# A later place for the mLSTM's output splits, and two more PSUM banks for the input projection

## The chip, the cores and the metric

The kernel runs on one core of a Trainium2 chip. The metric is the device time of one execution in microseconds. TensorE does matrix products into PSUM (8 banks of 128 partitions x 512 fp32 values), VectorE and ScalarE read PSUM and work elementwise, GpSimd helps with elementwise work on SBUF, and SyncE (SP) issues the DMAs. The page calls the engines PE (its weight loads PEld), DVE, ACT, POOL and SP.

## What is computed

One layer of a streaming encoder on a sequence of 1024 tokens with 1024 features, in fp32:

```
x = x + 0.5 * swiglu_ffn(x, ffn1...)
h = rms_norm(x, mix_norm)
(aq, ak, av, iq, ik, iw, mx, mv, mi, mf, mo, ga, gb) = split_columns(h @ w_in)
ya = dsa_attention(q, k, v, iq, ik, iw)      # top-k keys by an indexer's score, then softmax
yb = mlstm_branch(mx, mv, mi, mf, mo, ...)   # matrix memory, chunk by chunk, gated by mo
merged = sigmoid(ga) * (ya @ w_proj_a) + sigmoid(gb) * (yb @ w_proj_b)
x = x + merged @ w_out
x = x + 0.5 * swiglu_ffn(x, ffn2...)
```

## The kernel before

Every fp32 product is made of three faster ones: each operand is split into a rounded part hi and a rest lo (ScalarE copies hi, VectorE or GpSimd subtracts for lo), and `mm3` (lines 831 to 833) adds hi x hi, hi x lo and lo x hi in PSUM. The products with large weights follow a scheme of 2x2 blocks with seven products in place of eight.

The input projection h @ w_in is the generator `mixing`. Its work is a written-out list, `MIXING`, of items (p, q): p is a pair of 128-column blocks of w_in (MX0, MX1, MV0, MV1, AKV, AQ0, AQ1, G_A[0], G_A[1], MO0, MO1, G_B[3], and at last G_A[2] and G_A[3] together), q one of the seven products. An item is 12 matmuls of 128x512 (four steps of `mm3`) into one bank. Products 0 and 1 of a pair share a bank, 5 and 4 as well, and 6 and 3; the second of each adds to what the first left, after VectorE or ScalarE has read the first's sum. A middle pair runs in the order 5, 6, 1, 4, 2, then product 0 of the next pair, then 3. G_A[2] and `LAST` = G_A[3] run side by side in the order 0, 1, 5, 4, 6, 3, 2. The token operands lie in SBUF pages named h (products 0, 1, 2, 6), swap (5, 4) and side (3).

An item that begins a bank takes the first of the list `self.banks`, and one that ends a bank appends it: a queue of free banks. It holds four: 0, 1, 6 and 7. Banks 2 and 3 serve transposes and small products, and banks 4 and 5 hold the output of the mLSTM's current chunk (`out` in `mlstm`), and later attention's scores.

The weights of an item are loaded into a page "raw", then split into one of four pairs of slots in the page "round" by ScalarE (line 570) and GpSimd (571); with `LOOK = 3` the split of an item is written three items ahead, just before the matmuls of the third item before it. Products 5, 6, 4, 2 of some pairs come ready split from DRAM (567).

Beside the projection run other generators: the mLSTM scan over eight chunks (`mlstm`), and the top-k search for attention (`topk`, lines 1605 to 1699, mostly VectorE). `pump` moves the projection by half an item, counts a tick, and calls what `later(n, f)` has put n ticks ahead. `mlstm` pumps as it goes, and returns four items short of (G_A[1], 3). Hooks are called behind certain items of `LAST`. Behind (LAST, 1) `load_yb` starts the loads of the mLSTM's gated output (eight blocks of 128x512, line 1979, one a tick), and four ticks behind each load `halves` splits the block into the page h0 (ScalarE line 960, VectorE 961). Behind (LAST, 4) the query loads are written (2107), behind (LAST, 3) the key loads (2112).

Then attention follows. In its gaps `proj_b` multiplies the split output with w_proj_b (loads of its gate at line 2000, the sums times the gate at 2007, weight splits at 191).

The order in each engine's queue is not the order of the source. The program is built with `schedule_with_timeline_sim=True`: a planner runs through an estimate of its own, and gives an engine that comes free one of the instructions that are ready by the estimate, the earliest in the source first. On the chip each queue then runs in the order so fixed. A tile's buffers are taken from SBUF in source order, the one that has been free longest first.

Lines of use below: 1268 is the sum of a finished corner in `mixing` (VectorE), 1302 the sum behind product 5, 1307 the one behind product 4, 1266 and 1275 ScalarE's copies behind products 1 and 0, 1940 the scaling of a chunk's output in `mlstm` (the last reader of banks 4 and 5), 1966 the gating of the mLSTM's output (`gated`), 2043 the normed keys in `keys_norm`, 2055 the stores of the keys to `d_kg`, 1409 the stores of gates.

Of the kernel before, what the change touches and what calls it, by code (L numbers as in the profile page):

```python
# [744 lines left out]
class Block:  # L745
# [1225 lines left out]
    def load_yb(self):  # L1971

        nc = self.nc
        self.segment("h0", None)
        self.ybT = [[None, None] for _ in range(4)]
        def part(i):
            th, h = i // 4, i % 4
            t = self.ar.alloc(512)
            nc.sync.dma_start(t.f, self.d_yb[h, :, th * 512:th * 512 + 512])

            def halves():
                hi, lo = self.take("h0", 512), self.take("h0", 512)
                self.split(hi.r, lo.r, t.f)
                t.free()
                self.ybT[h][th] = hi, lo
            self.later(4, halves)


        for i in range(8):
            self.later(i, lambda i=i: part(i))  # L1990

# [330 lines left out]
    def run(self, x, out):  # L2322
# [66 lines left out]
        def used(*qs):  # L2389
            for q in qs:  # L2390
                for pair in T[q]:
                    for b in pair:
                        b.free()
# [9 lines left out]
        def third_used():  # L2403
            used(3)
            self.key_loads()
            self.w.prime(3, 1)

        self.hooks = {(LAST, 1): first_used, (LAST, 4): sums_used, (LAST, 2): lambda: used(6, 2),
# [14 lines left out]
        self.pump_waiting()  # L2423
        self.rq = ar.alloc(64, keep=True)
        self.mlstm((G_A[1], 3))
        self.pump_past((G_A[1], 3))
        assert not self.waiting
        self.close("extra")
# [76 lines left out]
```

## Time and profile before

| | |
|---|---|
| median of 3 runs | 2098.55 us (2096.47 to 2101.47) |
| the profiled execution | 2095.19 us, span 2093.1 us |
| TensorE clock granted over it | 0.996 of full |
| TensorE busy | 2035.2 us, 97% |
| VectorE busy | 1615.8 us, 77% |
| ScalarE busy | 1047.7 us, 50% |
| GpSimd busy | 303.3 us, 14% |
| DMA, share of 16 engines | 52.4% on SP's queue, mean 175 GB/s |

Busy time counts an instruction's own span. A matmul's shown duration overlaps the next one's, so a steady stream of 128x512 products is read from its starts. The span runs from the first instruction to the last; the execution's time has 2.1 us around it. The mLSTM's last chunks, the projection's end and the start of attention lie between 1060 and 1200 us of the span. The granted clock of TensorE is given as a share of full speed: 1.00 is 2.4 GHz, 0.50 is 1.2 GHz.

### The profile page before, as it was taken

The page shows a single profiled execution, that of the slowest core. Times are in us where ns is not written, and L with a number is a line of the kernel's source. Part 1 is how long each engine was busy: PE and PEld are TensorE (multiplying, and loading weights), DVE is VectorE, ACT ScalarE, POOL GpSimd, SP SyncE. Part 2 cuts the span into 40 slices and gives each one's busy share as a digit, 9 for nine tenths or more (in the row PEclk, how much of TensorE's full clock was granted, in tenths as well). Part 3 has the DMA queues.
Part 4 walks back from the last instruction along what each step waited for, and adds up shares of the span by engine and source line. Part 5 has one row for each costly group of instructions (what it writes and reads, how often), then busy time and mean ns, then how long its engine had stood idle before and what let it go on. Part 6 is the DMA issues. An engine that isn't in the chain of part 4 may idle for free.

```text
span 2093.1 us, 27987 instructions
## 1 busy us (share of the span) xinstructions
PE 2035.2 (97%) x9341; PEld 1669.1 (80%) x9341; DVE 1615.8 (77%) x2847; ACT 1047.7 (50%) x1961; POOL 303.3 (14%) x353
## 2 busy tenths in 40 slices
PE   7999999999999989999998999999999999999999
PEld 5788887888887777788787788788888888888887
DVE  7987888979866576988888489798976676669863
ACT  8332433334437566976775378636533333334442
POOL 1000000000004222223523445322000000000000
PEclk9999999999999999999999999999999999999999
DMA  5477778895543262576676912832332323386331
GB/s 187 128 247 225 255 258 280 275 362 183 174 185 136 56 192 86 156 219 196 200 254 212 324 51 70 299 115 96 123 125 101 111 97 105 107 294 247 126 111 40
DMA packets 286604, 366.63 MB, mean 175 GB/s; under 512 B 22924, under 2 KB 172028, under 8 KB 286332
## 3 DMA queue, kind: packets, MB, share of 16 engines
q1 hardware_dynamic: 286460, 364.85, 52.4%
q8 instruction: 73, 1.20, 0.2%
q14 instruction: 71, 0.58, 0.1%
HBM read 245.72 MB, written 119.05 MB: 174 GB/s over the span
## 4 chain that ended last, share of the span: by engine, by line
PE 52%; DVE 5%; DMA 4%; ACT 2%; issue 1%; SPq 0%; POOL 0%; DVEq 0%; ACTq 0%; POOLq 0%
PE psum L832 15%; PE psum L831 15%; PE psum L833 15%; PE psum L2161 1%; PE psum L1535 1%; PE psum L1536 1%; PE psum L2216 1%; PE psum L2215 1%; DMA round<-d_s 1%; DMA extra<-d_w 1%; DVE plain L1646 0%; DMA d_tb<-plain 0%; DVE plain L1565 0%; DVE h L961 0%; ACT plain L1676 0%
## 5 line engine op out<-in xcount | busy, mean ns | idle before, releaser
L831 PE MATMUL psum<-h,round 128*128 128x512 f32 x656 | 260.9, 399 | 5.6 <-ACT round L570 2.7
L832 PE MATMUL psum<-h,round 128*128 128x512 f32 x656 | 258.7, 395 | 1.0 <-DVE h L961 0.8
L833 PE MATMUL psum<-h,round 128*128 128x512 f32 x656 | 257.6, 394 | 0.8 <-POOL round L571 0.5
L831 PEld LDWEIGHTS psum<-h,round 128*128 128x128 f32 x656 | 123.8, 189 | 33.8 <-ACT round L570 3.7
L833 PEld LDWEIGHTS psum<-h,round 128*128 128x128 f32 x656 | 123.6, 188 | 28.3 <-issue 1.4
L832 PEld LDWEIGHTS psum<-h,round 128*128 128x128 f32 x656 | 124.0, 189 | 26.5 <-DVE h L961 1.6
L831 PE MATMUL psum<-swap,round 128*128 128x512 f32 x328 | 131.0, 400 | 6.7 <-DVE plain L1648 2.0
L833 PE MATMUL psum<-swap,round 128*128 128x512 f32 x328 | 131.1, 400 | 0.5 <-POOL round L571 0.5
L832 PE MATMUL psum<-swap,round 128*128 128x512 f32 x328 | 130.0, 396 | 0.8 <-DVE swap L961 0.6
L571 POOL TENSOR_TENSOR round<-raw,round 128x512 fp32r<-128x512 f32 x73 | 102.4, 1409 | 163.0 <-ACT round L570 137.9
L1646 DVE TENSOR_SCALAR_CACHE_REDUCE plain<-plain 128x384 bf16<-128x384 f32 (+1 forms) x124 | 107.7, 868 | 2.1
L960 ACT ACTIVATE round<-plain 128x512 fp32r<-128x512 f32 x73 | 45.7, 631 | 99.1 <-PE psum L832 93.8
L303 ACT ACTIVATE round<-plain 128x512 fp32r<-128x512 f32 x75 | 46.9, 631 | 89.9 <-PE psum L832 60.7
L833 PE MATMUL psum<-h,extra 128*128 128x512 f32 x212 | 82.5, 390 | 1.5 <-POOL extra L571 1.5
L831 PEld LDWEIGHTS psum<-swap,round 128*128 128x128 f32 x328 | 62.7, 192 | 23.2 <-ACT plain L1677 2.4
L831 PE MATMUL psum<-side 128*128 128x512 f32 x208 | 80.9, 389 | 0.0
L832 PE MATMUL psum<-side 128*128 128x512 f32 x208 | 80.9, 389 | 0.0
L833 PE MATMUL psum<-side 128*128 128x512 f32 x208 | 80.9, 389 | 0.0
L832 PE MATMUL psum<-h,spare 128*128 128x512 f32 x196 | 76.6, 391 | 1.9 <-DVE h L961 1.9
L831 PE MATMUL psum<-h,extra 128*128 128x512 f32 x192 | 75.0, 391 | 3.3 <-DVE plain L1123 3.3
L914 POOL MEMSET raw<- 128x384 f32 x1 | 0.4, 419 | 533.0 <-DMA d_o<-plain 533.0
L831 PE MATMUL psum<-h,spare 128*128 128x512 f32 x196 | 76.8, 393 | 0.4 <-ACT h L960 0.4
(770 smaller groups left out, 5916.1 us busy)
## 6 DMA issues: line engine op xcount, KB each, us to landing
plain<-d_a SPq DMA_DIRECT2D x154, 256.0 KB
d_a<-plain SPq DMA_DIRECT2D x126, 256.0 KB
d_s<-plain SPq DMA_DIRECT2D x93, 256.0 KB
raw<-in_ffn_w_gate_dram SPq DMA_DIRECT2D x44, 512.0 KB
h<-in_ffn_w_down_dram SPq DMA_DIRECT2D x66, 256.0 KB
plain<-in_w_in_dram SPq DMA_DIRECT2D x32, 512.0 KB
round<-d_s SPq DMA_DIRECT2D x64, 256.0 KB
raw<-in_w_in_dram SPq DMA_DIRECT2D x57, 256.0 KB
```

The costliest lines, as they stand in the source:

```text
L303: k.nc.scalar.activation(hi.r.rearrange("p (k c) -> p k c", k=4), src, AF.Copy)
L571: k.nc.gpsimd.tensor_tensor(lo.r, raw.f, hi.f, ALU.subtract)
L831: mm(ps, lhs[0], rhs[0], start=start, stop=False, skip_group_check=more)
L832: mm(ps, lhs[0], rhs[1], start=False, stop=False, skip_group_check=more)
L833: mm(ps, lhs[1], rhs[0], start=False, stop=stop, skip_group_check=more)
L960: self.split_A = self.nc.scalar.activation(hi, src, AF.Copy).ins
L1535: self.nc.tensor.matmul(o, qb, khi.r[:, s * n:s * n + n], start=True, stop=False)
L1536: last = self.nc.tensor.matmul(o, qb, klo.r[:, s * n:s * n + n], start=False, stop=True).ins
L1646: v.tensor_scalar(s.junk[:, :s.width[j]], s.sc[j], one(s.cand, j), one(s.neg, j), ALU.is_ge, ALU.add, accum_out=one(s.cnt, j))
L2161: self.last = nc.tensor.transpose(ps[:, j * P:(j + 1) * P], pr[j].f[:, kt * P:(kt + 1) * P], self.ident).ins
L2215: mm(po, vr[:, kt, g, :], hi.r, start=kt == 0, stop=False)
L2216: mm(po, vr[:, kt, g, :], lo.r, start=False, stop=kt == b)
```

## The change

Two things. The eight `halves` are no longer put four ticks behind their loads; they are collected in `self.yb_halves` and called in the hook of (LAST, 3), behind the key loads and ahead of the weights of the next stage. Only two items of the projection come after this hook in the source, (G_A[2], 2) and (LAST, 2), and their weights are split by then. And when `mlstm` returns, banks 4 and 5 are appended to the projection's queue of free banks, which then holds six.

```diff
@@ load_yb
                 self.ybT[h][th] = hi, lo
-            self.later(4, halves)
+            self.yb_halves.append(halves)
 
+        self.yb_halves = []
         for i in range(8):
             self.later(i, lambda i=i: part(i))
@@ run
         def third_used():
             used(3)
             self.key_loads()
+            for halves in self.yb_halves:
+                halves()
             self.w.prime(3, 1)
@@ run
         self.mlstm((G_A[1], 3))
+
+        self.banks += [4, 5]
         self.pump_past((G_A[1], 3))
```

## Rows read from the trace of the kernel before

**Rows 1.** The page, its first lines: the span, then busy us of each engine.
```profile
span 2093.1 us, 27987 instructions
PE 2035.2 (97%) x9341; PEld 1669.1 (80%) x9341; DVE 1615.8 (77%) x2847; ACT 1047.7 (50%) x1961; POOL 303.3 (14%) x353
```

**Rows 2.** Windows: stretch, its us, busy us (instructions) by engine, clock, DMA, GB/s.
```profile
1100.00:1120.00 20.00, 20.00 (x90) 16.57 (x89) 19.97 (x30) 14.56 (x29) 4.07 (x3) 1.00 0.77 252
1120.00:1140.00 20.00, 17.85 (x80) 13.66 (x79) 19.96 (x21) 7.14 (x13) 13.24 (x7) 1.00 0.34 106
...
1180.00:1200.00 20.00, 16.76 (x75) 12.99 (x74) 8.93 (x19) 6.38 (x11) 7.03 (x11) 1.00 0.82 292
```

**Rows 3.** TensorE's timeline: start, us, line, operands; in brackets idle before and its releaser.
```profile
1004.93 0.47 PE L831 MATMUL psum<-swap,round 128*128 128x512 f32 x1 [2.02 <-DVE plain L1648]
...
1065.65 0.39 PE L831 MATMUL psum<-swap,round 128*128 128x512 f32 x1
...
1071.09 0.39 PE L831 MATMUL psum<-h,round 128*128 128x512 f32 x1
...
1125.35 0.47 PE L831 MATMUL psum<-h,round 128*128 128x512 f32 x1 [1.20 <-DVE plain L837]
...
1145.97 0.47 PE L831 MATMUL psum<-swap,round 128*128 128x512 f32 x1 [1.36 <-DVE plain L1302]
...
1148.57 0.39 PE L833 MATMUL psum<-swap,round 128*128 128x512 f32 x1
1151.64 0.80 PE L831 MATMUL psum<-h,round 128*128 128x512 f32 x1 [2.69 <-ACT round L570]
```

**Rows 4.** ScalarE's timeline; between the first two rows five more splits of line 960.
```profile
1147.84 0.63 ACT L960 ACTIVATE h<-more 128x512 fp32r<-128x512 f32 x1 [2.81 <-DMA more<-d_yb]
...
1150.98 1.66 ACT L570 ACTIVATE round<-raw 128x512 fp32r<-128x512 f32 x3
...
1156.59 0.63 ACT L960 ACTIVATE h<-spare 128x512 fp32r<-128x512 f32 x1 [3.95 <-DMA spare<-d_yb]
```

**Rows 5.** The chain that ended last, from 1136 to 1152: start, us, what.
```profile
1142.09 5.72 DMA more<-d_yb
```

**Rows 6.** Windows around the wait before 1151.64; columns as in rows 2.
```profile
1149.00:1151.60 2.60, 0.00 (x0) 0.00 (x0) 2.60 (x5) 2.60 (x6) 0.00 (x0) 0.91 1.05 406
1151.60:1153.00 1.40, 1.36 (x3) 1.16 (x4) 1.20 (x3) 1.03 (x2) 1.33 (x2) 0.50 1.05 405
1153.00:1155.00 2.00, 2.00 (x7) 1.54 (x6) 1.09 (x2) 0.00 (x0) 2.00 (x2) 0.61 1.06 388
```

**Rows 7.** VectorE's timeline, columns as in rows 3.
```profile
1071.29 0.69 DVE L1302 TENSOR_TENSOR more<-spare,psum 128x512 f32<-128x512 f32 x1 [0.39 <-PE psum L833]
...
1073.33 0.69 DVE L1940 TENSOR_TENSOR spare<-psum,plain 128x512 f32<-128x512 f32 x1
...
1081.99 0.75 DVE L1966 SCALAR_TENSOR_TENSOR spare<-more,par,spare 128x512 f32<-128x512 f32 x1 [1.33 <-ACT spare L1965]
...
1089.61 0.75 DVE L1966 SCALAR_TENSOR_TENSOR plain<-plain,par 128x512 f32<-128x512 f32 x1 [1.98 <-DMA plain<-d_h]
...
1124.55 0.65 DVE L1307 TENSOR_TENSOR more<-more,psum 128x512 f32<-128x512 f32 x1
...
1131.29 2.25 DVE L2043 TENSOR_TENSOR plain<-plain 128x1024 f32<-128x1024 f32 x1
...
1151.81 0.69 DVE L1302 TENSOR_TENSOR spare<-plain,psum 128x512 f32<-128x512 f32 x1 [0.20 <-DMA d_kg<-spare]
...
1175.09 0.69 DVE L2007 TENSOR_TENSOR plain<-plain,psum 128x512 f32<-128x512 f32 x1 [2.03 <-PE psum L833]
```

**Rows 8.** SP's timeline of DMA issues, from 1150 to 1160.
```profile
1153.04 1.04 SPq L2000 DMA_DIRECT2D plain<-d_tb  x2
...
1156.95 2.92 SPq L2107 DMA_DIRECT2D swap<-d_aq  x4
```

## The prediction

> **What bounds the kernel now.** The page comes first: one core, a span of 2093.1 us, TensorE busy for 97% of it [rows 1]. A gain can only come from stretches in which TensorE stands still, so I read the windows by stage for the part that the diff touches, from the mLSTM's last chunks (about 1060 us) to the start of attention (about 1175 us). From 1100 to 1140 us VectorE is busy for 39.9 of 40 us, while TensorE falls from 20.00 to 17.85 us in the second half [rows 2]: the end of the input projection is bound by VectorE, which still finishes the top-k search, and TensorE has slack there. Then the list of TensorE's waits, and the timeline for what ended each. Three of them matter [rows 3]: 1.20 us before 1125.35, 1.36 us before 1145.97, 2.69 us before 1151.64.
>
> The last one ends with a weight split: the first of the three L570 that start at 1150.98 ends at 1151.6. In front of them on ScalarE stand six splits of the mLSTM's output (L960), and the first of these had waited 2.81 us for its load [rows 4], which was issued at 1142.09 and took 5.72 us [rows 5]. After the wait the clock is at half: a granted share of 0.50 over 1.40 us and of 0.61 over 2.00 us [rows 6], a loss of 0.50 x 1.40 + 0.39 x 2.00 = 1.5 us. So this place holds 2.7 + 1.5 = 4.2 us, 0.2% of the time, which is also about what a measurement of this kernel can tell from no change.
>
> **Part one, the splits.** Nothing is added or removed: eight splits, each one L960 on ScalarE and one L961 on VectorE, move from four half steps behind their loads to the hook of (LAST, 3). They stay hidden: 8 x 0.63 = 5 us of ScalarE, which stands idle 3.95 us before 1156.59 alone [rows 4], and the first product that needs them is multiplied at 1175.09 [rows 7]. Without that cover they would cost up to 5 us at the start of attention. The loads stay where they are, and no DMA changes its place. Eight 128x512 buffers are held until the hook, but the destinations of the two L1302 that matter below are allocated before any of the eight was freed, so those stay as they are.
>
> The question is whether the move in the source moves them in the queue. A queue's order is the planner's, which gives a free engine whatever is ready by its estimate; the source only sets who goes first among the ready. The trace shows how far it reaches: on SP the loads of proj_b (L2000) stand at 1153.04, before the query loads (L2107) at 1156.95 [rows 8], which the source has first, in the hook of (LAST, 4). And it shows that the place in the source did not put the six L960 first: with `LOOK = 3` the split of the weights of (G_A[2], 6) is written before the matmuls of (LAST, 5), the first two `halves` behind them. It had the better claim and stands behind all six, so by the estimate it wasn't ready (it needs the slots of (G_A[2], 5)) and ScalarE was free. A lower claim for the six doesn't change that. I take 0 us for part one; the other bound is that the order does change.
>
> If it does, something else is late next. (G_A[2], 4) ends at 1148.57 + 0.23 = 1148.8 [rows 3]. Of the items behind it, (LAST, 4) needs the second L1302, which waited until 1151.81 for the d_kg store to leave its destination and ends at 1152.5 [rows 7]. If the planner fills the time with all of (G_A[2], 6) and then (LAST, 6), the whole 4.2 us are won; the 1.36 us before 1145.97 stay, since they end with the first L1302. If it keeps the present order, four matmuls of (G_A[2], 6) and then (LAST, 4), TensorE waits until 1152.6 all the same, and (LAST, 4) is done 12 x 0.227 = 2.7 us later at 1155.3, or 1156.8 with the half clock; now it is done by 1156.95, when the loads that overwrite its operand start [rows 8]. So: -4.2 to 0 us.
>
> **Part two, the banks.** They are appended when the mLSTM returns, four items short of (G_A[1], 3). At that point two of the projection's four banks are free; (G_A[1], 2) and (MO0, 0) take those, and the next two, banks 4 and 5, go to (MO0, 5) and (MO0, 6). Both still hold the last chunk's output: it is read until L1940 ends at 1073.33 + 0.69 = 1074.0 [rows 7], while (MO0, 5) starts at 1065.65 [rows 3]. So the change adds a wait at the mLSTM's end. Queued behind it on TensorE is the rest of the projection; the four pairs of weight slots let only (G_A[1], 3) and (MO0, 1) pass it, 24 matmuls at (1071.09 - 1065.65) / 24 = 0.227 us [rows 3], done by 1071.1. Then TensorE stands until 1074.0: 2.9 us. The low bound: without the L1302 of (MO0, 5) before it (0.69 us and a wait of 0.39 us [rows 7]) L1940 can end at 1072.9, which leaves 1.8 us. The high bound adds the half clock, 1.5 us, as after the wait of 2.69 us, behind which a matmul took 0.80 us; behind the 2.02 us before 1004.93 it took 0.47 us [rows 3]. So 1.8 to 4.4 us late; I take 3, nearest to L1940's row.
>
> What becomes of it: VectorE follows TensorE there, but stood idle 1.33 us before 1081.99 and 1.98 us before 1089.61 [rows 7]; 3.0 - 3.3 leaves about 0 for VectorE, and at most 4.4 - 3.3 = 1.1. (The second of these is a wait for the mLSTM's last output, whose transposes can now run earlier, in the gap.) TensorE's own delay runs into its waits for VectorE, 1.2 + 1.4 us up to 1146, and then into the 2.7 us at the splits. So the 3 us are absorbed, and the end moves by VectorE's shift, 0 to 1.1 us; I take 0.5.
>
> The gain: the wait before 1125.35 is one for a bank. (LAST, 0) takes the one that (G_B[3], 4) gave back, which the L1307 at 1124.55 still reads (L837 right behind it is only the last VectorE instruction done by then) [rows 3, 7]. With two more banks it goes, 1.2 us. But L2043, whose product TensorE transposes next, ends at 1131.29 + 2.25 = 1133.5 on a VectorE that is full [rows 2, 7], so TensorE only waits longer there: I take 0, with 1.2 as the other bound.
>
> The Trainium skill, "TensorE: Matmul & The Clock Gate", section "HAM oscillation — how this bites in real kernels", tells of a kernel in which double-buffering PSUM, on top of a mended feed, gave no further gain; that speaks against the banks. By it this term is 0, by the row 1.2 us. The 0 in the sum comes from L2043, and the sum stands without the page.
>
> **Sum.** 0 (splits) + 0.5 (wait at the mLSTM's end) - 0 (bank wait) = +0.5 us on an execution of 2095.2 us (span 2093.1 [rows 1] and 2.1 around it). The median of the runs, 2098.55, stands 3.4 us above that execution, so 2099 us.
>
> **Rivals.**
> *Queue kept, wait absorbed* (0.58), as worked out; with the runs' own spread 2096 to 2102 us. In it the first half of the diff does not do what it says.
> *The splits do leave ScalarE's way* (0.24). For it: the chain of waits goes from the d_yb load through the L960 to L570 and TensorE [rows 4, 5]. Against it: the planner's order, and the second L1302. -4.2 us, and with the bank's 1.2 us -5.4: 2093 to 2098 us, 2095 in the middle.
> *The new wait is not absorbed* (0.18), the one on the slower side. If the planner expects L1940 late, it puts more of the top-k search ahead of VectorE's reads of (MO0, 5) and what follows; the idle 3.3 us are then used up before TensorE's delay arrives, and a full VectorE [rows 2] carries the rest to the end. It decides once VectorE is more than 3.3 us late. Against it: the search was paced by the projection's own sums so far. +1.8 to +4.4 us, and 1.5 us more if a later wait halves the clock again: 2100 to 2105 us.
>
> The range, 2093 to 2104 us, holds all but the ends of the second and third. Beside these three, the planner also rewrites attention's queues, whose first 20 us hold 3.2 us without TensorE [rows 2]; that may be won or lost again, and I give it a sixth of the first case, half to each side. Faster by over 0.2% (4.2 us): the better two thirds of the second and the lucky part of the first, 0.16 + 0.05 = 0.21. Slower by as much: the upper two thirds of the third and the unlucky part, 0.12 + 0.05 = 0.17, which I round to 0.20 for mechanisms that I don't see. Within: 0.59.
>
> **What would show it.** Right: ScalarE still runs L960 ahead of L570 near 1148, and TensorE waits there; (MO0, 5) starts behind L1940, after a TensorE wait of 2 to 3 us near 1072; no bank wait near 1125 and a longer one for L2043. Wrong: L570 ahead of the L960 and no wait over 1 us from 1145 to 1160 (the second rival); VectorE full from 1080 on and every later wait at its old length (the third); or other waits in attention, which I hold fixed.

## The result

The change makes the kernel slower: 2108.6 us median of 5 runs (2105.19 to 2113.88) against 2096.47 us for the kernel before on the same chip (5 runs, 2091.11 to 2101.47). The ratio is 1.0056, with a 95% interval of 1.0030 to 1.0082: 11.7 us, 6 to 17. The profiled execution is the longest of the five, 2113.88 us.

**Profile after.** Line numbers below the first hunk are two higher than before (L2000 is L2002, L2043 is L2045). First the page's span and busy times, against [rows 1].

```profile
span 2111.9 us, 27973 instructions
PE 2042.6 (97%) x9341; PEld 1673.6 (79%) x9341; DVE 1618.7 (77%) x2847; ACT 1048.7 (50%) x1961; POOL 300.8 (14%) x353
```

The span is 18.8 us longer. Some of that was there before the touched code was reached. TensorE's timeline after begins with a row that answers to the first one of [rows 3]; up to this point both kernels have the same instructions in the same order.

```profile
1011.98 0.47 PE L831 MATMUL psum<-swap,round 128*128 128x512 f32 x1 [2.03 <-DVE plain L1648]
...
1069.62 0.60 PE L1385 MATMUL psum<-ident,more 128*128 128x128 f32 x4
...
1080.41 0.63 PE L1385 MATMUL psum<-ident,spare 128*128 128x128 f32 x4 [1.99 <-DVE spare L1940]
...
1088.24 0.50 PE L831 MATMUL psum<-swap,round 128*128 128x512 f32 x1 [1.73 <-DVE more L1302]
...
1143.83 1.09 PE L1385 MATMUL psum<-ident,plain 128*128 128x128 f32 x8 [0.97 <-DVE plain L2045]
...
1156.05 0.47 PE L831 MATMUL psum<-swap,round 128*128 128x512 f32 x1 [1.19 <-DVE plain L1302]
...
1161.63 0.68 PE L831 MATMUL psum<-h,round 128*128 128x512 f32 x1 [2.58 <-ACT round L570]
...
1185.10 1.07 PE L1535 MATMUL psum<-side,swap 128*128 128x512 f32 x4
...
1187.95 0.50 PE L1535 MATMUL psum<-side,swap 128*128 128x512 f32 x1 [0.87 <-DVE plain L2149]
1190.63 0.70 PE L1535 MATMUL psum<-side,swap 128*128 128x512 f32 x2 [1.49 <-DVE plain L2153]
1191.83 0.73 PE L1536 MATMUL psum<-side,swap 128*128 128x512 f32 x2 [0.49 <-DMA side<-d_kg]
1194.24 0.77 PE L1535 MATMUL psum<-side,swap 128*128 128x512 f32 x1 [1.33 <-DMA swap<-d_aq]
1198.13 0.80 PE L1535 MATMUL psum<-side,swap 128*128 128x512 f32 x1 [1.84 <-DVE plain L2149]
...
1362.80 0.80 PE L832 MATMUL psum<-swap,round 128*128 128x512 f32 x1 [0.65 <-DVE swap L961]
```

The wait for L1648 ends at 1011.98 in place of 1004.93 [rows 3], so about 7 us belong to this execution and not to the change. To leave them out, I measure two stretches between rows that every variant has: from the mLSTM's transposes (the L1385 at 1069.62) to attention's first score (L1535), and from there to a wait of the merge behind attention (the L832 at 1362.80). The same three rows of TensorE's timeline before, and two of its waits there that are compared below:

```profile
1062.44 0.60 PE L1385 MATMUL psum<-ident,more 128*128 128x128 f32 x4
...
1133.60 1.09 PE L1385 MATMUL psum<-ident,plain 128*128 128x128 f32 x8 [0.28 <-DVE plain L2043]
...
1174.89 1.07 PE L1535 MATMUL psum<-side,swap 128*128 128x512 f32 x4
...
1196.75 0.50 PE L1535 MATMUL psum<-side,swap 128*128 128x512 f32 x1 [2.07 <-DVE plain L2147]
...
1343.00 0.80 PE L832 MATMUL psum<-swap,round 128*128 128x512 f32 x1 [0.58 <-DVE swap L961]
```

The projection's end went from 112.45 to 115.48 us (+3.0), attention from 168.11 to 177.70 us (+9.6). The sum, 12.6 us, is what the runs measure within their interval. Three quarters of it lie in attention, whose own code the diff does not touch. (A program that was traced twice, e1 and e3 below, gave -0.2 and -0.3 us for the first stretch and +9.5 and +9.0 for the second; so the stretches of one execution are good to about half a microsecond, where the order of the instructions is the same.)

**The projection's end.** The predicted wait is there: 1.99 us for L1940, behind which (MO0, 5) follows, then a second one of 1.73 us for the L1302 that reads (MO0, 5). The bank wait before 1125 is gone, and TensorE waits longer for the normed keys (0.97 us against 0.28 in the same place before). ScalarE runs in the old order:

```profile
1157.83 0.63 ACT L960 ACTIVATE h<-more 128x512 fp32r<-128x512 f32 x1 [2.57 <-DMA more<-d_yb]
...
1160.96 1.65 ACT L570 ACTIVATE round<-raw 128x512 fp32r<-128x512 f32 x3
```

The six splits still stand ahead of the weight split, and TensorE still waits 2.58 us there [rows 3, 4].

**Attention's start.** SP's issues of proj_b's first two gate loads, and the first sum that needs one (VectorE), after:

```profile
1175.59 0.32 SPq L1409 DMA_DIRECT2D d_sa<-plain  x1
1175.96 0.42 SPq L2002 DMA_DIRECT2D plain<-d_tb  x1
...
1185.76 0.32 SPq L1409 DMA_DIRECT2D d_sa<-plain  x1
1186.95 0.32 SPq L2002 DMA_DIRECT2D plain<-d_tb  x1
```
```profile
1199.13 0.68 DVE L2009 TENSOR_TENSOR plain<-plain,psum 128x512 f32<-128x512 f32 x1
```

Before, both loads were issued at 1153.04 [rows 8] and the first sum ran at 1175.09 [rows 7]. With the 10 us by which everything is later at this point (the L570 wait ends at 1161.63, before at 1151.64), the loads are some 13 and 24 us late and the sum 14. In VectorE's queue the sum now stands behind five score reductions (L2149); before, it stood ahead of the first. By the order of allocations in the source, the first load now gets the buffer out of which a gate of G_A[2] is stored (L1409), the second the one of G_A[2]'s sum behind product 5 (L1302): both are in use until the projection's end. proj_b has one bank, so its second block of 12 matmuls waits for that sum. In the kernel before the blocks of proj_b stood between the score pairs; now only scores are left there, and TensorE waits five times within 11 us: by the rows above three of these waits end with VectorE, which has to read the banks of earlier scores, and two with loads of the keys (`side`) and queries (`swap`). The clock falls. Windows after, columns as in [rows 2]:

```profile
1185.00:1190.00 5.00, 3.27 (x14) 2.05 (x12) 2.05 (x3) 1.33 (x2) 0.27 (x2) 1.00 1.02 414
1190.00:1195.00 5.00, 2.55 (x8) 1.58 (x9) 1.89 (x6) 2.11 (x3) 2.74 (x4) 0.75 1.00 370
1195.00:1200.00 5.00, 3.16 (x8) 1.96 (x7) 3.31 (x7) 2.09 (x5) 1.65 (x3) 0.50 1.05 379
1200.00:1205.00 5.00, 5.00 (x19) 4.13 (x18) 1.47 (x4) 2.36 (x4) 3.60 (x4) 0.73 0.91 287
```

The theory from this (A): the late splits do nothing to ScalarE's queue, but they give their eight input buffers back later in the source, so that the gate loads are handed other buffers, which come free late; and the wait for L1940 is carried to the end. Its rival (B): the banks do it all, since attention's scores meet other banks.

### The profile page after: what moved, and what is told of

Same layout as the page of the kernel before. It is cut to its first block, busy times and chain, and to the rows that moved or that the text cites. A ratio compares the mean times of both kernels' runs of the same rounds, so it can differ in the third digit from the quotient of the medians.

```text
span 2111.9 us, 27973 instructions
## 1 busy us (share of the span) xinstructions
PE 2042.6 (97%) x9341; PEld 1673.6 (79%) x9341; DVE 1618.7 (77%) x2847; ACT 1048.7 (50%) x1961; POOL 300.8 (14%) x353
## 4 chain that ended last, share of the span: by engine, by line
PE 52%; DVE 6%; DMA 4%; ACT 2%; issue 1%; POOL 0%; SPq 0%; DVEq 0%; ACTq 0%; POOLq 0%
PE psum L831 15%; PE psum L832 15%; PE psum L833 15%; PE psum L2163 1%; PE psum L1535 1%; PE psum L1536 1%; PE psum L2218 1%; PE psum L2217 1%; DVE plain L1646 1%; DMA extra<-d_w 1%; DMA d_sa<-plain 1%; DVE plain L1565 0%; DVE h L961 0%; ACT plain L1676 0%; DMA d_h<-extra 0%
## 5 line engine op out<-in xcount | busy, mean ns | idle before, releaser
L832 PE MATMUL psum<-h,round 128*128 128x512 f32 x656 | 259.3, 396 | 1.0 <-DVE h L961 0.8
L832 PEld LDWEIGHTS psum<-h,round 128*128 128x128 f32 x656 | 124.4, 190 | 26.8 <-DVE h L961 1.5
L832 PE MATMUL psum<-swap,round 128*128 128x512 f32 x328 | 130.1, 397 | 0.9 <-DVE swap L961 0.7
L571 POOL TENSOR_TENSOR round<-raw,round 128x512 fp32r<-128x512 f32 x73 | 100.6, 1383 | 167.4 <-ACT round L570 142.0
L960 ACT ACTIVATE round<-plain 128x512 fp32r<-128x512 f32 x73 | 45.7, 631 | 99.6 <-PE psum L832 94.3
L832 PE MATMUL psum<-side 128*128 128x512 f32 x208 | 80.9, 389 | 0.0
L832 PE MATMUL psum<-h,spare 128*128 128x512 f32 x196 | 76.6, 391 | 1.9 <-DVE h L961 1.9
```

What stands on the lines that cost most here:

```text
L571: k.nc.gpsimd.tensor_tensor(lo.r, raw.f, hi.f, ALU.subtract)
L832: mm(ps, lhs[0], rhs[1], start=False, stop=False, skip_group_check=more)
L960: self.split_A = self.nc.scalar.activation(hi, src, AF.Copy).ins
```

## The experiments

Eleven kernels ran, each in five rounds beside the kernel before. A time is a median, the ratio to the kernel before stands with its 95% interval, and a time with a sign that stands with a ratio is the ratio's distance from 1 times 2096 us. Such a time and the difference of the medians can differ by up to 2 us (e1: 6.9 and 8.0; e6: 6.9 and 5.0).

**e1, the splits alone.** The first two hunks of the diff, without the banks.

> Only the splits' part of the diff: the eight halves go to the hook of (LAST, 3), the banks stay four. Theory A (buffers): the eight input buffers of the splits are given back later in the source, so the first two gate loads of proj_b get other buffers, which come free some 20 us later; proj_b's products then can't fill the score waits at attention's start. It expects +6 to +10 us against the kernel before, ScalarE's order at 1148 unchanged, no wait at the mLSTM's end, the second gate load issued near 1177 in place of 1153. Theory B (the banks do it all; the prediction's 0 for this part): 0 us, within 2 us of the kernel before.

2103.76 us, ratio 1.0033 (1.0023 to 1.0043): +6.9 us. Projection's end -0.2 us, attention +9.5 us in the profiled execution. The first gate loads are issued at 1164.89 and 1176.27. Windows of e1 at attention's start:

```profile
1175.00:1180.00 5.00, 2.56 (x11) 1.47 (x9) 2.54 (x5) 1.60 (x3) 0.82 (x3) 1.00 1.03 415
1180.00:1185.00 5.00, 3.63 (x10) 1.90 (x8) 1.57 (x5) 2.41 (x4) 2.18 (x3) 0.61 1.03 392
1185.00:1190.00 5.00, 3.95 (x10) 3.17 (x10) 4.41 (x9) 2.58 (x5) 3.08 (x6) 0.50 1.08 375
1190.00:1195.00 5.00, 5.00 (x23) 4.04 (x22) 0.85 (x2) 1.45 (x3) 2.15 (x2) 0.86 0.72 201
```

The clock alone costs 0.39 x 3.63 + 0.50 x 3.95 + 0.14 x 5.00 = 4.1 us here. B's 0 for this part falls.

**e2, the banks alone.**

```diff
         self.mlstm((G_A[1], 3))
+        self.banks += [4, 5]
         self.pump_past((G_A[1], 3))
```

> Only the banks' part of the diff: banks 4 and 5 appended when the mLSTM returns, the splits as before. Theory A: only the wait for L1940 at the mLSTM's end counts, of which about 1 us is absorbed: +2 to +4 us, with gaps of some 2.0 and 1.7 us near 1073 to 1085 and attention's first 20 us as in the kernel before. Theory B: the whole loss of the change, +9 to +12 us, attention's first waits included, because its score pairs meet other banks.

2102.77 us, ratio 1.0031 (1.0019 to 1.0043): +6.5 us (4.0 to 9.0), between the two theories. Projection's end +4.3 us, attention +3.6 us. With e1's 6.9 it makes 13.4, and the change measured 11.7 (6 to 17): within the intervals the two parts add up.

**e3, only the frees.**

```diff
                 self.split(hi.r, lo.r, t.f)
-                t.free()
                 self.ybT[h][th] = hi, lo
             self.later(4, halves)
+            self.yb_in.append(t)
@@ third_used
             self.key_loads()
+            for t in self.yb_in:
+                t.free()
```

> The kernel before with its splits in their old place; only the giving back of their eight input buffers is put off to the hook of (LAST, 3). Theory A: the same as with the splits moved, +6 to +10 us, since only the buffers matter. Theory B: 0 us.

2104.24 us, ratio 1.0035 (1.0023 to 1.0047): +7.3 us, the same as e1. Compared instruction by instruction, e1 and e3 are the same program: all five queues have the same instructions in the same order, with the same operands and waits. Moving the splits in the source did nothing but move the frees.

**e5, two buffers handed over.** e1, with the inputs of parts 1 and 2 kept for proj_b's first two gates: by the order of allocations in the source these are the buffers that the gate loads had in the kernel before.

```diff
+                if i in (1, 2):
+                    self.gate_in.append(t)
+                else:
+                    t.free()
@@ proj_b
-                s = self.ar.alloc(512)
+                s = self.gate_in.pop(0) if self.gate_in else self.ar.alloc(512)
```

> The splits in the hook of (LAST, 3) as in e1, but two of their input buffers, those that the first two gate loads of proj_b got in the kernel before, are handed to these loads. Theory A (buffers): the +8 us of e1 go, -2 to +2 us against the kernel before, the first gate load issued near 1153 again. Theory B (the late splits themselves, or the other six buffers): still +6 to +9 us.

2096.03 us, ratio 0.9995 (0.9985 to 1.0006): the loss is gone. Attention is at +0.1 us. SP's issue of both gate loads in e5, whose execution is 3.4 us later than that of the kernel before at the mLSTM's transposes, so that this answers to 1153.04:

```profile
1156.13 0.83 SPq L2005 DMA_DIRECT2D plain<-d_tb  x2
```

Within the interval, two buffers out of eight are the whole of the splits' loss.

**e6, the whole change with the same two buffers handed over.**

> The whole change, with the same two buffers handed to the first two gate loads. Theory A: the splits' part is taken out, the banks' part stays as in e2: +4 to +8 us against the kernel before. Theory B (the two parts aren't separate): +10 to +12 us, as the change.

2101.89 us, ratio 1.0033 (1.0021 to 1.0044): what is left is e2's loss. Projection's end +3.9 us, attention +2.4 us.

**e4 and e10, the banks later.**

```diff
# e4
         self.pump_past((G_A[1], 3))
+        self.banks += [4, 5]
# e10
         self.mlstm((G_A[1], 3))
+        self.pump_past((G_A[1], 4))
+        self.banks += [4, 5]
         self.pump_past((G_A[1], 3))
```

> The kernel before with banks 4 and 5 appended four items later, behind (G_A[1], 3): they then go to (MO1, 0) and (MO1, 5), long after L1940. Theory A: no wait at the mLSTM's end, and the bank wait before 1125 is gone, whose 1.2 us L2043 takes back: -1 to +1 us. Theory B: the same other banks in attention as with the early append, +8 to +11 us.

> Banks 4 and 5 appended behind (G_A[1], 4), one item after the mLSTM's return: (MO0, 5) keeps its old bank, (MO0, 6) gets bank 4, and the transposes of the last chunk pass ahead of it. Theory A (the wait for L1940 makes the whole loss of the banks' part, attention's share too): -1 to +2 us, no wait near 1073. Theory B' (six banks in other places disturb attention by themselves): +3 to +6 us without that wait.

e4: 2096.41 us, ratio 0.9998 (0.9989 to 1.0007). Six banks without the wait cost nothing and win nothing: projection's end -0.5 us, attention +0.1 us. The bank wait before 1125 is gone, and what stands in its place is the wait that was expected there:

```profile
1136.24 1.09 PE L1385 MATMUL psum<-ident,plain 128*128 128x128 f32 x8 [1.08 <-DVE plain L2043]
```

e10: ratio 1.0008 (0.9996 to 1.0021), which decides nothing between its two expectations. There is no wait for L1940, and attention is at -0.2 us, so other banks do not disturb attention by themselves. But the projection's end is at +3.8 us in this execution, with other waits, and attention does not suffer from beginning late:

```profile
1117.31 0.50 PE L833 MATMUL psum<-swap,round 128*128 128x512 f32 x1 [1.83 <-DMA round<-d_s]
...
1129.90 0.50 PE L831 MATMUL psum<-side,round 128*128 128x512 f32 x1 [1.84 <-DVE plain L1268]
```

**e7 and e8, the splits really behind the weights.** In e7 each split of `halves` is tied in the planner to the last weight split written by then; its buffers stay as before. e8 adds e4's later banks.

```diff
-                self.split(hi.r, lo.r, t.f)
+                with self.tc.issue_after(self.mp.done_A):
+                    self.split(hi.r, lo.r, t.f)
```

> The kernel before, with each of the eight splits tied in the planner behind the last weight split that was written by then, buffers and places in the source unchanged, so that L570 of (G_A[2], 6) stands ahead of the first L960 on ScalarE. Theory C (the six splits are what TensorE waits for at 1149 to 1151.6): the wait of 2.7 us and the half clock behind it go, -4 to -2 us. Theory D (behind them stands the second L1302, whose destination the d_kg stores hold until 1151.8, and TensorE waits for (LAST, 4) then): 0 us, within 1 us.

> e7 and e4 together: the splits tied behind the weight splits, and banks 4 and 5 appended behind (G_A[1], 3). Theory C: -5 to -2 us, as the slack that the banks give no longer ends at the weight split. Theory D: 0 us, within 1 us.

e7: ratio 0.9996 (0.9985 to 1.0006); e8: 0.9995 (0.9985 to 1.0005). L570 does stand ahead of L960 now, and the time is the same (e7: -0.8 us, -3.1 to +1.3). ScalarE, VectorE and TensorE of e7:

```profile
1149.57 0.64 ACT L570 ACTIVATE round<-raw 128x512 fp32r<-128x512 f32 x1
1153.14 0.63 ACT L960 ACTIVATE h<-more 128x512 fp32r<-128x512 f32 x1 [2.93 <-DMA more<-d_yb]
```
```profile
1157.21 0.69 DVE L1302 TENSOR_TENSOR spare<-plain,psum 128x512 f32<-128x512 f32 x1 [2.11 <-DMA d_kg<-spare]
```
```profile
1150.26 0.50 PE L831 MATMUL psum<-h,round 128*128 128x512 f32 x1 [1.00 <-ACT round L570]
...
1157.95 0.50 PE L831 MATMUL psum<-swap,round 128*128 128x512 f32 x1 [2.15 <-DVE spare L1302]
```

TensorE runs on into (G_A[2], 6) and then waits 2.15 us for the second L1302, whose destination the key stores leave late. That is theory D; the mild end of C's range would pass by the time alone, and it is the trace that rules C out: the wait moved to the second L1302.

**e9 and e11, that buffer too.** e9 reserves the destinations of the two L1302 early; e11 is e9, e7 and e4 together.

```diff
-                s["u2"], goes_on = ar.alloc(512), "x2"
+                s["u2"], goes_on = self.u2.pop(0) if p in G_A[2:] else ar.alloc(512), "x2"
@@ run
         self.pump_past((MO1, 3))
+        self.u2 = [ar.alloc(512) for _ in range(2)]
```

> The kernel before, with the two sums behind product 5 of (G_A[2], 5) and (LAST, 5) (the two L1302 that waited for stores to leave their destinations) in two buffers reserved behind (MO1, 3). If the buffers of these sums bound the projection's end: the wait of 1.4 us before (G_A[2], 4) goes and the splits' stall with the half clock behind it shrinks, -5 to -2 us. If TensorE then only waits for the next thing in the same place (the loads of the mLSTM's output ahead of L570): -1 to +1 us.

> The reserved buffers for the two sums, the splits tied behind the weight splits, and the banks appended behind (G_A[1], 3), together: each of the three things that TensorE met between 1125 and 1152 is taken away. If their places were what bound the projection's end: -6 to -3 us against the kernel before. If L2043 on VectorE and the loads under a full DMA share only take their place: -2 to 0 us.

e9: ratio 0.9989 (0.9979 to 1.0000), -2.3 us, at the edge of the noise. e11: 2095.38 us against 2097.24, ratio 0.9986 (0.9977 to 0.9996), -2.9 us, between its two expectations and clear of the noise by little. Its trace does not show where that would come from: in e11's profiled execution the projection's end is at -1.0 us, with new waits of 1.57 us for an L1275 and 1.31 us for an L1268, and attention at +1.6. e9's projection ends 3.6 us earlier; attention gives 1.8 us back, where TensorE now waits for the key loads. TensorE of e9:

```profile
1173.10 1.82 PE L1535 MATMUL psum<-side,swap 128*128 128x512 f32 x4 [2.20 <-DMA side<-d_kg]
```

## Why the prediction was wrong

The forecast was 2099.0 us, "queue kept, wait absorbed"; the time is 2108.6, beyond the range and beyond the rival on the slower side.

**Part one, 0 us: the step that failed.** That the queue keeps its order was right (L960 ahead of L570 after; e1 and e3 the same program). But the cover was asked only of the splits and of two destinations: "the destinations of the two L1302 that matter below are allocated before any of the eight was freed, so those stay as they are", and "no DMA changes its place". Among the next tiles taken after the frees are the gates of proj_b. Their loads stand in [rows 8] and their first sum in [rows 7], and I used both rows for other ends. Handed two other buffers, the loads moved by 13 and 24 us. This term was +6.9 us in place of 0 (e1), and e5, with -1.0 us (-3.1 to +1.3), shows that the two buffers are all of it.

**The wait for L1940: right in place and size.** One wait, 1.8 to 4.4 us late, was the forecast, 3 the value taken; it came as two, of 1.99 and 1.73 us. In e2 the second wait is missing and the clock is at half behind the first instead (0.70 and 0.50 in the windows from 1075 to 1079), for about the same sum.

**"Absorbed": the second step that failed.** The 3.3 us for which VectorE stood idle were to swallow the delay. One of the two idle times did vanish, but a new one came. VectorE after, against [rows 7]:

```profile
1084.01 0.75 DVE L1966 SCALAR_TENSOR_TENSOR spare<-more,par,spare 128x512 f32<-128x512 f32 x1 [1.77 <-ACT spare L1965]
...
1096.14 0.74 DVE L1966 SCALAR_TENSOR_TENSOR plain<-plain,par 128x512 f32<-128x512 f32 x1
...
1110.71 0.69 DVE L1307 TENSOR_TENSOR plain<-plain,psum 128x512 f32<-128x512 f32 x1 [2.65 <-PE psum L833]
...
1141.52 2.25 DVE L2045 TENSOR_TENSOR plain<-plain 128x1024 f32<-128x1024 f32 x1
```

The wait of 1.98 us before the L1966 is gone, and VectorE now waits 2.65 us for TensorE before an L1307. The idle time moved, it was not used up: from the mLSTM's transposes to the normed keys VectorE stands idle 5.19 us, before 4.50. That stretch (to L2045) takes 71.90 us (1141.52 - 1069.62), before 68.85 (1131.29 [rows 7] - 1062.44): VectorE is late by 3.05 us, as much as the projection's end. It is 2.36 us late at the L1307 (1101.17 before), whose start TensorE sets. The other 0.69 us come behind it, where VectorE does not wait at all, but some of the same instructions take longer: an L1626 takes 1.93 us in place of 0.87, with a weight split of GpSimd (L571) running from 1117.76 to 1119.36 beside it, where none ran before. The prediction held these durations fixed, and no run separates this part. So the later waits of TensorE hardly shrank: 1.19 and 2.58 us against 1.36 and 2.69 [rows 3]. The first ends with VectorE; the second ends with a weight split behind a load that was itself issued 2.8 us later (82.45 us behind the mLSTM's transposes, before 79.65). The third rival had this outcome with "+1.8 to +4.4 us", and the projection's end measured +3.0, +4.3 and +3.9 us (after, e2, e6). Its reason was another: it had VectorE full from 1080 on, and VectorE waits 2.65 us.

**The bank wait, 0 of 1.2 us: right** (e4). The Trainium skill ("TensorE: Matmul & The Clock Gate", section "HAM oscillation — how this bites in real kernels"), whose kernel gained nothing further from double-buffered PSUM, agrees with e4's ratio of 0.9998.

**The rival that the splits leave ScalarE's way: its price was wrong, its doubt right.** -4.2 us were given for it, 0 if the second L1302 stands behind. In e7 it does: TensorE waits 2.15 us for it.

**Attention "held fixed"** was named as what could go wrong, at a sixth of the first case. It took 9.6 of 12.6 us. Each part alone, the buffers make 9.5 us there (e1) and the banks 3.6 (e2), or 2.4 beside the handed-over buffers (e6). That is more than 9.6 together, so the shares inside the whole change are not settled: the buffers' may be anything from 6.0 to 9.5 us. What makes the banks' share stays open. Other banks alone don't make it (e4 +0.1, e10 -0.2), and a late arrival alone doesn't either: e10's projection ends 3.8 us late and its attention takes as long as before. Nor is it shown how the late gates lead to the 2.9 us more of waits at attention's end (6.5 us from 1313 to 1363 after, 3.6 us from 1327 to 1343 before).

## What to carry to other kernels

Where a step moves in the source, follow what it frees as well as what it issues: the next owner of each buffer, until one of them has a DMA on the path. An idle time did not absorb a delay here, because the idle engine was itself fed by the delayed one; ask, for each idle time that you count on, who feeds that engine. And before pricing a wait that is to go, look at what stands right behind it: here a store that held a buffer stood behind the queue, and a load some 20 us on, so that the queue alone won nothing and the buffer alone about 2 us, at the edge of the noise.

## What the runs showed of the hardware

In the splits' part the clock and the waits share the loss about evenly. Windows over the whole of attention, the kernel before and then e1, columns as in [rows 2]:

```profile
1174.89:1343.00 168.11, 160.19 (x869) 132.42 (x867) 136.81 (x354) 126.45 (x274) 79.77 (x139) 1.00 0.39 139
```
```profile
1174.03:1351.59 177.56, 165.18 (x870) 135.30 (x868) 138.02 (x355) 128.98 (x279) 79.42 (x139) 0.96 0.41 141
```

The same products keep TensorE busy 5.0 us longer, at a granted share of 0.96 in place of 1.00, and it stands still 4.5 us longer (12.4 us in place of 7.9). In the kernel before, one wait of 2.07 us near 1196 leaves the granted clock at 1.00 in its windows of 5 us, at a DMA share of 0.16 and 0.23. In e1 five waits of 0.5 to 1.6 us between 1176 and 1187, with DMA at a full share, go with 0.61 and then 0.50 in the windows of 5 us shown above. TensorE of e1:

```profile
1176.88 0.50 PE L1535 MATMUL psum<-side,swap 128*128 128x512 f32 x1 [0.87 <-DVE plain L2149]
...
1179.65 0.70 PE L1535 MATMUL psum<-side,swap 128*128 128x512 f32 x2 [1.57 <-DMA side<-d_kg]
1180.82 0.97 PE L1536 MATMUL psum<-side,swap 128*128 128x512 f32 x2 [0.47 <-DMA side<-d_kg]
...
1183.12 0.80 PE L1535 MATMUL psum<-side,swap 128*128 128x512 f32 x1 [0.90 <-DVE plain L2149]
...
1186.24 0.80 PE L1535 MATMUL psum<-side,swap 128*128 128x512 f32 x1 [1.05 <-DVE plain L2149]
```

No run here tells apart how much the number of the waits and how much the DMA share has to do with it; a full DMA share alone leaves the clock at 1.00 (before, 1175 to 1185: a share of 1.03, TensorE never idle).

Over whole runs the mean granted clock of e1 is 0.9916 (8 runs) against 0.9945 (26 runs of the kernel before). By an estimate that takes TensorE as always busy, 0.0029 of 2096 us is 6.1 us of e1's 6.9; this also counts a lowered clock in which TensorE waits, and so may be too high. In the banks' part the clock has the smaller share: e2's mean is 0.9937, by the same estimate 1.7 of its 6.5 us.
